# Roots on ACT, residual adds by DMA, a fourth split-weight buffer and a re-ordered norm 2 in a one-core transformer block

## The chip, the cores and the metric

The kernel runs on one core of a Trainium2 chip. The metric is the device time of one execution in microseconds (us); the kernel before was timed in three runs. The engines are called as in the profile: PE multiplies matrices (its weight loads are listed as PEld), DVE does vector work out of on-chip memory and the matmul banks, ACT evaluates functions and copies, POOL does a little arithmetic and issues DMAs that may accumulate into their destination, and SP issues plain DMAs.

## The reference, cut to what matters

512 tokens of 1024 channels, all float32, one layer, one batch entry:

```
h  = rmsnorm(x, norm1_g) * (1 + scale1) + shift1
qa, ka, va, qd, kd, vd, ga, gd = split(h @ w_in)
out_a = sliding-window attention (8 heads, window 128, sinks)
out_d = differential attention (4 heads, two softmax maps), per-head rmsnorm
x  = x + gate1 * ((sigmoid(ga) * (out_a @ w_branch_swa) + sigmoid(gd) * (out_d @ w_branch_diff)) @ w_out)
h2 = rmsnorm(x, norm2_g) * (1 + scale2) + shift2
a, g = split(h2 @ w_up)                 # 1024 -> 2 x 2816
a  = causal conv of width 3 along the tokens, per channel, + conv_b
x  = x + gate2 * ((gelu(a) * g) @ w_down)   # 2816 -> 1024
out = rmsnorm(x, final_g)
```

`scale`, `shift` and `gate` are six rows that come from the conditioning vector `c` (`silu(c) @ w_ada + b_ada`).

## The kernel before, in words

**Split products.** A float32 matrix is multiplied as a high part (a cast to the matmul type, on ACT) and a low part (the difference, on DVE), and each product is three matmuls: high·high, high·low, low·high. So every weight block costs one cast on ACT (line 102 or 990) and one subtraction on DVE (line 103 or 994) before PE can use it. The two parts of a weight lie in rotating buffers with the tags `whi` and `wlo`, `WB` = 3 of each; a new split has to wait until PE is done with the block three before.

**Stages.** In order of time: norm 1 and the first projections (to about 60 us), the two attentions (to 235), the branch projections and gates (to 305), the output projection with norm 2 (to 351), the MLP's up projection (to 578; PE line 1051, matmuls of 128x256), the down projection (to 683.6; PE line 1651, matmuls of 128x512), and the tail.

**Seven products for eight.** Both MLP projections work on a 2 x 2 blocking of their operands with seven block products (p1, m5, m6, p2, m7, p3, p4) of sums of blocks, for eight plain ones. Blocks that are needed as sums are made by DMAs on POOL's queue that accumulate into a loaded block, or by DVE (`sum_w`).

*Up.* `J` counts 11 pairs of column tiles; `mul_slot(J, name)` multiplies one of the seven, `cast_w` and `low_w` split its weight, `behind` takes the result out of its bank, and `conv_taps` and `conv_gelu` do the convolution and GELU. For J = 0 and 1 the order of DVE, ACT, PE and POOL is written out by hand, from the last steps of the output projection on (`out_step`): row by row, `add_x` adds the residual, `square2` sums squares on ACT, `norm_a` and `norm_b` make the root, `norm_c` scales the row; then PE transposes (bank names `th`) and the row is modulated (`early`). The splits of the weights p1 and p2 of pair 1 (`hi_early`, `lo_early`) are placed between these. From J = 2 on a scheduler sets the order.

*Down.* Seven passes over the 2816 channels in six groups (`grp`, five of two tiles and one of one), in the order m1, m5, m6, p2, p3, m7, p4, 66 matmuls each. `prepare(i, g)` splits the weight block and the activation block of a group, and for m1, m5, m6 and p3 then issues an accumulating DMA that turns the weight block (`chain` or `b`) into the one which a later pass needs. In the trace, `b<-in_w_down_dram` on POOL's queue is such a DMA for pass m7: it is issued when p3's split of the same block is done. The results lie in four pairs of banks (dX, dZ, dY, dW). After a pass its results are taken out by small DVE tasks (`after_pass`), handed out over the groups of the next pass by the table `EACH`. p4 accumulates onto dW, the bank that m7 has filled, so its first matmul waits until DVE has taken m7's result out of it (line 1525).

**Residual and last norm.** The tasks multiply by the gate, add into the residual `x1` (`res(t, hf)`: row tile t, half hf) with a DVE addition, sum the squares of the half on ACT (`square`, line 1488), and multiply by the final gain (`fgb`). `stat_start` and `stat_end` make the root of a row.

**Roots.** `rstd_start` raises the mean square to the power −0.5 on POOL (line 143), and `rstd_end` does a refinement step in two DVE operations of 128x1 (lines 149 and 153).

**The tail** (`last_rows`) holds back the last three groups of p4. Row tile 2 is finished first. Then row tile 3 in two halves of 256 columns, `c0` and `c1`, of one bank: all of c0's matmuls, then all of c1's. DVE multiplies by the gate (line 1563), adds (1566), ACT squares (1569), DVE applies the gain (1573), the root follows, and the scaled row goes out in two DMAs, the last one on ACT's queue (1585).

Of the kernel before, what the change touches and what calls it, by code (L numbers as in the profile page):

```python
# [14 lines left out]
P = 128  # L15
# [10 lines left out]
DIFF_HEADS = 4  # L26
WB = 3
HP = 100000
# [15 lines left out]
def kernel(  # L44
# [101 lines left out]
    def rstd_end(dst, ms, r0, n, wpool):  # L146
        t = wpool.tile([P, n], F32, tag="rs_b", bufs=3, name="rt")
        if n == 1:
            nc.vector.scalar_tensor_tensor(t, r0, r0, ms, ALU.mult, ALU.mult)
# [706 lines left out]
    while units or loaded or current or later:  # L856
        fill(1)
    for _ in ada:
        fill(1)
# [259 lines left out]
    def square2(t, hfs=(0, 1)):  # L1119
        for hf in hfs:  # L1120
            sq = big.tile([P, S], F32, tag="sq2", name=f"sqo{t}{hf}")
            ssq[t, hf] = bp.tile([P, 1], F32, tag="ss2", bufs=8, name=f"sso{t}{hf}")
            nc.scalar.activation(sq, x1[:, t, hf * S : (hf + 1) * S], AF.Square, accum_out=ssq[t, hf])  # L1123

    def norm_a(t):
        nc.vector.tensor_scalar(ssq[t, 0], ssq[t, 0], 1.0 / D, EPS, ALU.mult, ALU.add)
        r2[t] = rstd_start(ssq[t, 1], 1, D, bp, plus=ssq[t, 0])

    def norm_b(t):
        rs = bp.tile([P, 1], F32, tag="rs2", bufs=4, name=f"rso{t}")  # L1130
        rstd_end(rs, *r2[t], 1, bp)
        xns[t] = xnp[t // 2][:, t % 2]
        return rs
# [74 lines left out]
    square2(1)  # L1208
    lo_early(2, q0)
    norm_a(1)  # L1210
    lo_early(2, q1)
    norm_c(1, norm_b(1))
# [34 lines left out]
    norm_halves(2, norm_b(2))  # L1247
    norm_halves(3, norm_b(3))
    early(2, "lo")
# [19 lines left out]
    mul_slot(0, "p2", (0,))  # L1269
    cast_w(0, "m5")  # L1270
    for g in (0, 1):
# [7 lines left out]
    bV += [tbank("up6"), tbank("up7")]  # L1279
    low_w(0, "m5")  # L1280
    for q in (q0, q1):
        V.tensor_sub(t1n[:, q], b11[:, q], b12[:, q])
    sum_w(0, "m6")
    hi_t(0, t1n, q0)
# [12 lines left out]
    behind(0, "p1")  # L1297
    nc.scalar.copy(bh[:, 2], b22)
    low_w(0, "m6")
    lo_t(1, t1n, q0)  # L1300
# [32 lines left out]
    mul_slot(1, "m6")  # L1333
    behind(1, "m5")
    conv_bias(0, 1)
    conv_taps(0, 0)
    sum_w(1, "p3")
    conv_taps(0, 1)
    cast_w(1, "p3")
    conv_gelu(0, 0)  # L1340
    behind(1, "m6")
    cast_w(1, "m7")
    low_w(1, "p3")
    mul_slot(1, "p3")
    conv_gelu(0, 1)
    low_w(1, "m7")
    mul_slot(1, "m7")
    load_a(2, 0)
    cast_w(2, "p1")
    behind(0, "c22")  # L1350
    behind(0, "p4")
    behind(1, "p2")
    low_w(2, "p1")
    mul_slot(2, "p1")
    behind(1, "p3")
    cast_w(1, "p4")
    conv_bias(1, 0)
    conv_bias(1, 1)
    low_w(1, "p4")
    behind(1, "m7")  # L1360
    mul_slot(1, "p4")
    load_s1(2)
    load_a(2, 1)
    load_s3(2)
    load_a22(2)
    conv_taps(1, 0)
    cast_w(2, "m5")
    conv_gelu(1, 0)
    low_w(2, "m5")
    sum_w(2, "m6")  # L1370
    behind(2, "p1")
    conv_taps(1, 1)
    cast_w(2, "m6")
    conv_gelu(1, 1)
    low_w(2, "m6")
    behind(1, "c22")
    behind(1, "p4")
    cast_w(2, "p2")
    low_w(2, "p2")
    man.close()  # L1380
# [110 lines left out]
    def stat_start(t):  # L1491
        a, b = parts[t, 0], parts[t, 1]
        nc.vector.tensor_scalar(a, a, 1.0 / D, EPS, ALU.mult, ALU.add)
        parts[t] = rstd_start(b, 1, D, bp, plus=a)

    def stat_end(t):
        rs = bp.tile([P, 1], F32, tag="rs2", bufs=4, name=f"rsd{t}")
        rstd_end(rs, *parts[t], 1, bp)
        return rs
# [4 lines left out]
    def gate(hf):  # L1504
        return g2b[hf]


    def after_pass(name):
# [14 lines left out]
        elif name == "m7":  # L1523
            for u in two:
                yield lambda u=u: V.tensor_sub(e2[:, u], e2[:, u], dW[u])
            for u in two:
                yield lambda u=u: V.tensor_mul(e2[:, u], e2[:, u], gate(1))
            for u in two:
                def add(u=u):
                    V.tensor_add(res(2 + u, 1), res(2 + u, 1), e2[:, u])  # L1530
                    square(2 + u, 1)
                yield add
            for u in two:
                def gain(u=u):
                    V.tensor_mul(e2[:, u], res(2 + u, 1), fgb[:, S:])
                    stat_start(u)
                yield gain
        elif name == "p3":
            for u in two:
                yield lambda u=u: V.tensor_sub(e[:, u], e[:, u], dZ[u])  # L1540
# [21 lines left out]
    def last_mul(u, sl=slice(0, S)):  # L1562
        nc.vector.tensor_mul(m1[:, u, sl], dW[u][:, sl], gate(0)[:, sl])

    def last_add(u, sl=slice(0, S)):
        nc.vector.tensor_add(res(2 + u, 0)[:, sl], res(2 + u, 0)[:, sl], m1[:, u, sl])
        sq = big.tile([P, S], F32, tag="sq2", name=f"sqe{u}_{sl.start}")
        s1 = bp.tile([P, 1], F32, tag="ss2", bufs=8, name=f"sse{u}_{sl.start}")
# [18 lines left out]
    def last_rows(todo):  # L1587
# [53 lines left out]

    def multiply(i, g, u, sl=slice(0, S)):
        name, bank2 = passes[i][:2]
# [3 lines left out]
        for q in range(n):  # L1647
            first_mm = name in first and g == 0 and q == 0
            last_mm = g == len(grp) - 1 and q == n - 1
            for x, (a, b) in enumerate(((ah, wh), (ah, wl), (al, wh))):  # L1650
                nc.tensor.matmul(  # L1651
                    bank2[u][:, sl], a[:, q, cu], b[:, q, sl], start=first_mm and x == 0, stop=last_mm and x == 2,
                    skip_group_check=name not in first,
                )

    NG = len(grp)
    HOLD = 3
    EACH = {3: (0, 2, 2, 2, 1, 1), 4: (0, 0, 1, 1, 2, 2), 5: (0, 0, 2, 2, 2, 2), 6: (0, 0, 2, 2, 2, 2)}
    tasks = iter(())
    for i in range(len(passes)):  # L1660
        for g in range(NG):
            prepare(i, g)
            for _ in range(EACH.get(i, (0,) * NG)[g]):
                next(tasks)()
        tail = HOLD if i == len(passes) - 1 else 0
        for g in range(NG - tail):
            for u in range(2):
                multiply(i, g, u)
        if tail:
# [50 lines left out]
```

## Time and profile before

| | |
|---|---|
| three runs | 693.9 to 696.05 us, median 695.13 |
| profiled execution | 695.11 us, its span 693.3 |
| PE busy | 676.6 us (98%), 4117 matmuls |
| PEld busy | 591.5 us (85%) |
| DVE busy | 559.9 us (81%), 1028 instructions |
| ACT busy | 376.6 us (54%), 661 instructions |
| POOL busy | 72.7 us (10%), 81 instructions |
| DMA | 119.68 MB, mean 173 GB/s |

The busy times are of one execution. DVE's 81% is an average: it has stretches of 10 us in which it is full. In a row of a timeline the first number is the start in us, the second the busy time of the instruction, then engine, line, operation, the output and inputs by the program's names, and in brackets how long the engine stood before it and what released it. Operations on one engine overlap a little, so that the distance of two starts is shorter than the busy time of one.

### The profile page before, as it was taken

To read this page: it belongs to the slowest core of one execution; us is meant where nothing else is said; L and a number is where in the kernel's file an instruction comes from. 1 tells how busy PE (TensorE), PEld (TensorE's weight loads), DVE (VectorE), ACT (ScalarE), POOL (GpSimd) and SP (SyncE) were. 2 spreads that over 40 slices of the span, in tenths; PEclk is the share of its full clock that TensorE was granted. 3 is DMA by queue.
4 is the path that set the end of the run, shared out by engine and by line. 5 is a ranking of instruction groups with operands and counts; after the bars stand their busy time and mean duration, and the time that the engine had idled before them with its cause. 6 is when DMAs were issued, how large, how long until landed. Compare 5 with 4: busy or idle time off the path is not lost. (4 is left out here: it accounts for less than half of the span.)

```text
span 693.3 us, 10915 instructions
## 1 busy us (share of the span) xinstructions
PE 676.6 (98%) x4117; PEld 591.5 (85%) x4117; DVE 559.9 (81%) x1028; ACT 376.6 (54%) x661; POOL 72.7 (10%) x81
## 2 busy tenths in 40 slices
PE   8999999999999999999999999999999999999994
PEld 8787777778787888888799999999999998888873
DVE  4888887879787566663699898888888999979995
ACT  4656765354544333332487655665556565665663
POOL 2000000000100000000030101111111003431200
PEclk9999999999999999999999999999999999999997
DMA  9943544355254464258354988778867558996803
GB/s 351 407 166 108 185 134 151 122 172 158 97 178 156 142 222 152 93 186 245 115 108 133 217 212 197 188 194 185 204 172 185 140 177 204 196 205 182 144 1 122
DMA packets 71077, 119.68 MB, mean 173 GB/s; under 512 B 3952, under 2 KB 47728, under 8 KB 71024
## 3 DMA queue, kind: packets, MB, share of 16 engines
q1 hardware_dynamic: 52960, 95.04, 41.4%
q0 software_dynamic: 17776, 23.60, 20.6%
q8 instruction: 32, 0.52, 0.3%
q10 hardware_dynamic: 288, 0.34, 0.1%
q14 instruction: 21, 0.17, 0.1%
HBM read 116.87 MB, written 2.10 MB: 172 GB/s over the span
## 5 line engine op out<-in xcount | busy, mean ns | idle before, releaser
L1051 PE MATMUL up<-t,m_whi 128*128 128x256 f32 x528 | 96.1, 283 | 0.0
L1051 PEld LDWEIGHTS up<-t,m_whi 128*128 128x128 f32 x528 | 82.3, 192 | 0.0
L1051 PE MATMUL up<-t,m_wlo 128*128 128x256 f32 x264 | 74.6, 283 | 0.1
L1051 PE MATMUL up<-bh,p_wlo 128*128 128x256 f32 x232 | 65.7, 284 | 0.7 <-DVE p_wlo L994 0.7
L1051 PE MATMUL up<-bh,p_whi 128*128 128x256 f32 x232 | 65.6, 283 | 0.0
L1051 PE MATMUL up<-bl,p_whi 128*128 128x256 f32 x232 | 65.6, 283 | 0.0
L673 DVE CUSTOM_DVE_ANT_0 ra<-ra,csb 128x1024 f32<-128x1024 f32 x32 | 39.1, 1223 | 23.5 <-DMA ra<-in_w_ada_t_dram 23.2
L1051 PEld LDWEIGHTS up<-t,m_wlo 128*128 128x128 f32 x264 | 50.6, 192 | 0.3 <-DVE m_wlo L994 0.3
L1051 PEld LDWEIGHTS up<-bh,p_wlo 128*128 128x128 f32 x232 | 44.4, 192 | 1.1 <-DVE p_wlo L994 1.1
L1051 PEld LDWEIGHTS up<-bh,p_whi 128*128 128x128 f32 x232 | 44.5, 192 | 0.0
L1051 PEld LDWEIGHTS up<-bl,p_whi 128*128 128x128 f32 x232 | 44.5, 192 | 0.0
L962 POOL DMA_DIRECT2D s<-in_w_up_dram x21 | 27.1, 1363 | 156.0 <-DMA s<-in_w_up_dram 109.4
L143 POOL TENSOR_TENSOR r<-ms,mhalf 128x1 f32<-128x1 f32 (+1 forms) x13 | 11.8, 910 | 297.9 <-DVE ms L139 220.8
L994 DVE TENSOR_TENSOR m_wlo<-s,m_whi 128x1024 fp32r<-128x1024 f32 x31 | 37.8, 1220 | 2.0 <-ACT m_whi L990 2.0
L990 ACT CAST m_whi<-s 128x1024 fp32r<-128x1024 f32 x31 | 32.4, 1046 | 9.3 <-DVE s L984 6.0
L612 ACT ACTIVATE sd<-sd,dmx 128x128 f32<-128x128 f32 (+3 forms) x32 | 17.8, 556 | 29.8 <-DVE dmx L610 24.0
L1051 PE MATMUL up<-t,p_whi 128*128 128x256 f32 x176 | 32.2, 283 | 0.0
L1051 PEld LDWEIGHTS up<-t,p_whi 128*128 128x128 f32 x176 | 27.4, 192 | 0.2 <-issue 0.2
L1058 ACT ACTIVATE gT<-a,cols 128x512 f32<-128x512 f32 x22 | 17.7, 813 | 17.7 <-DVE a L1093 17.3
L990 ACT CAST p_whi<-wa 128x1024 fp32r<-128x1024 f32 x18 | 18.7, 1041 | 12.0 <-DMA s<-in_w_up_dram 8.9
L1051 PE MATMUL up<-t,p_wlo 128*128 128x256 f32 x88 | 24.9, 283 | 0.0
L994 DVE TENSOR_TENSOR p_wlo<-wa,p_whi 128x1024 fp32r<-128x1024 f32 x18 | 22.0, 1222 | 3.5 <-ACT p_whi L990 3.0
(497 smaller groups left out, 2010.0 us busy)
## 6 DMA issues: line engine op xcount, KB each, us to landing
ra<-in_w_ada_t_dram SPq DMA_DIRECT2D x32, 512.0 KB, 3.3
wa<-in_w_up_dram SPq DMA_DIRECT2D x22, 512.0 KB, 4.4
s<-in_w_up_dram SPq DMA_DIRECT2D x21, 512.0 KB, 4.7
s<-in_w_up_dram POOLq DMA_DIRECT2D x21, 512.0 KB, 6.1
adaw<-in_w_ada_t_dram SPq DMA_DIRECT2D x15, 512.0 KB, 9.8
a<-in_w_up_dram SPq DMA_DIRECT2D x11, 512.0 KB, 4.8
b<-in_w_down_dram SPq DMA_DIRECT2D x10, 512.0 KB, 4.3
w<-in_w_first_dram SPq DMA_DIRECT2D x8, 512.0 KB, 10.1
```

The costliest lines, as they stand in the source:

```text
L143: nc.gpsimd.tensor_tensor(r0, ms, mhalf[:, :n], ALU.pow)
L612: nc.scalar.activation(pm[m], pm[m], AF.Exp, bias=mx[:, m : m + 1], scale=slope, accum_out=lsum[:, m : m + 1])
L673: nc.vector.tensor_tensor_reduce(r, r, csb, 1.0, 0.0, ALU.mult, ALU.add, late_mod[:, idx : idx + 1])
L962: nc.gpsimd.dma_start(dst, upblock(*blk), accum_op=ALU.add)
L990: nc.scalar.copy(W[J, name][0], R[J, SRC[name]])
L994: nc.vector.tensor_sub(lo, R[J, SRC[name]], hi.bitcast(F32))
L1051: nc.tensor.matmul(o[u], w[:, k, cu], b[:, k], start=name in ("p1", "m5", "p2") and k == 0 and x == 0, stop=k == 3 and x == 2, skip_group_ ...
L1058: nc.scalar.activation(grow(j), av[J][:, u], AF.Identity, bias=cv[:, 66 + j : 67 + j], scale=cv[:, 44 + j : 45 + j])
```

## The change

- `WB` goes from 3 to 4: a fourth buffer for the high and the low part of split weights. The memory is taken from the area in which POOL's DMAs keep their descriptors (`dynamic_dma_scratch_size=8192`, which is 16384 without the argument).
- Roots of norm 2, of the last norm's rows and of the tail: ACT's Sqrt, then a reciprocal on DVE, for the power on POOL; the refinement step stays. Two more functions' tables are asked for ahead of time by a Sqrt or Gelu of one column (`root_table`, `warm`): Sqrt behind the last tanh of the gates, Gelu behind norm 2, Sqrt ahead of the down projection.
- Ahead of norm 2: the split of weight m5 of pair 0 and the second early cast come before the output projection's last steps; `lo_early(2)` is moved up by one row, and the sum for m6 takes its place. Further down in the hand-written order, casts, splits, convolution and GELU of J = 0 to 2 change places.
- Down projection: six residual additions of 128x512 on DVE (two each after p2, p3 and m7) become accumulating DMAs on POOL's queue from on-chip memory into `x1`; the square on ACT and the gain on DVE follow the DMA. After m7, two `row` tasks scale and send out the rows 0 and 1, which was done in the tail. The last groups of m7 and the first of p4 are multiplied one row tile at a time (`together`).
- Tail: the second half of row tile 3 is multiplied into a bank of its own (dY[1]); multiplications, additions, gain and scaling are ordered anew.

```diff
-WB = 3
+WB = 4
+    def root_start(ssq, d, wpool, plus):
+        r0 = wpool.tile([P, 1], F32, tag="rs_c", bufs=3, name="r0")
+        nc.scalar.activation(r0, ssq, AF.Sqrt, bias=plus, scale=1.0 / d)
+        ms = wpool.tile([P, 1], F32, tag="rs_a", bufs=3, name="ms")
+        nc.vector.scalar_tensor_tensor(ms, ssq, 1.0 / d, plus, ALU.mult, ALU.add)
+        return ms, r0
+
+    def root_end(dst, ms, r0, wpool):
+        nc.vector.reciprocal(r0, r0)
+        rstd_end(dst, ms, r0, 1, wpool)
+
+    def root_table(behind):
+        nc.scalar.activation(warm, behind, AF.Sqrt, scale=0.0)
...
+    root_table(tds[KT - 1][:, 0:1])
...
     hi_early(1)
     lo_early(1, slice(0, 4))
+    cast_w(0, "m5")
+    low_w(0, "m5")
+    hi_early(2)
     for k in last:
         out_step(0, k)
     add_x(0, 0)
     add_x(0, 1)
     square2(0)
+    lo_early(2, q0)
     norm_a(0)
+    lo_early(2, q1)
     norm_c(0, norm_b(0))
-    hi_early(2)
     for k in last:
         out_step(1, k)
     add_x(1, 0)
     add_x(1, 1)
     square2(1)
-    lo_early(2, q0)
+    sum_w(0, "m6")
     norm_a(1)
-    lo_early(2, q1)
     norm_c(1, norm_b(1))
...
     nc.scalar.copy(bh[:, 2], b22)
+    nc.scalar.activation(warm, rs_last, AF.Gelu, scale=0.0)
...
+    root_table(grow(FT - 1)[:, 0:1])
...
                 def add(u=u):
-                    V.tensor_add(res(2 + u, 1), res(2 + u, 1), e2[:, u])
+                    nc.gpsimd.dma_start(res(2 + u, 1), e2[:, u], accum_op=ALU.add)
                     square(2 + u, 1)
...
+            for u in two:
+                def row(u=u):
+                    nc.scalar.activation(x1[:, u], x1[:, u], AF.Copy, scale=stat_end(u))
+                    nc.sync.dma_start(od[u * P : (u + 1) * P, :], x1[:, u])
+                yield row
...
                 def add(u=u):
-                    V.tensor_add(res(u, 1), res(u, 1), e[:, u])
+                    nc.gpsimd.dma_start(res(u, 1), e[:, u], accum_op=ALU.add)
                     square(u, 1)
...
                 def add(u=u):
-                    V.tensor_add(res(u, 0), res(u, 0), m1[:, u])
+                    nc.gpsimd.dma_start(res(u, 0), m1[:, u], accum_op=ALU.add)
                     square(u, 0)
...
-        for sl in (c0, c1):
-            for g in todo:
-                multiply(len(passes) - 1, g, 1, sl)
-        for u in range(2):
-            nc.scalar.activation(x1[:, u], x1[:, u], AF.Copy, scale=stat_end(u))
-            nc.sync.dma_start(od[u * P : (u + 1) * P, :], x1[:, u])
-        last_mul(0)
-        s0 = last_add(0)
-        last_gain(0)
-        last_mul(1, c0)
-        r0 = rstd_start(s0, 1, D, bp, plus=part[0])
-        s1 = last_add(1, c0)
-        last_gain(1, c0)
+        for g in todo:
+            multiply(len(passes) - 1, g, 1, c0)
+        for g in todo:
+            multiply(len(passes) - 1, g, 1, c1, dY[1], g == todo[0])
+        last_mul(0, dW[0])
+        last_add(0)
+        s0 = last_square(0)
+        last_mul(1, dW[1])
+        r0 = root_start(s0, D, bp, part[0])
         rs0 = bp.tile([P, 1], F32, tag="rs2", bufs=4, name="rse0")
-        rstd_end(rs0, *r0, 1, bp)
+        root_end(rs0, *r0, bp)
+        last_add(1)
+        last_scale2(0, rs0, nc.sync)
+        s1 = last_square(1, c0)
+        nc.vector.scalar_tensor_tensor(res(2, 0), res(2, 0), rs0, fgb[:, :S], ALU.mult, ALU.mult)
+        nc.sync.dma_start(od[2 * P : 3 * P, :S], res(2, 0))
+        last_mul(1, dY[1], c1)
+        last_add(1, c1)
+        s2 = last_square(1, c1)
         partial(s1, part[1])
-        last_mul(1, c1)
-        s2 = last_add(1, c1)
-        r1 = rstd_start(s2, 1, D, bp, plus=s1)
-        last_gain(1, c1)
-        last_scale(0, rs0)
-        last_scale2(0, rs0, nc.sync)
+        last_gain(1)
+        r1 = root_start(s2, D, bp, s1)
         rs1 = bp.tile([P, 1], F32, tag="rs2", bufs=4, name="rse1")
-        rstd_end(rs1, *r1, 1, bp)
+        root_end(rs1, *r1, bp)
...
-    EACH = {3: (0, 2, 2, 2, 1, 1), 4: (0, 0, 1, 1, 2, 2), 5: (0, 0, 2, 2, 2, 2), 6: (0, 0, 2, 2, 2, 2)}
+    EACH = {3: (0, 2, 2, 2, 1, 1), 4: (0, 0, 1, 1, 2, 2), 5: (0, 0, 2, 2, 2, 2), 6: (0, 0, 2, 2, 3, 3)}
...
+        together = {"m7": (4, 5), "p4": (0, 1)}.get(passes[i][0], ())
         for g in range(NG - tail):
             for u in range(2):
-                multiply(i, g, u)
+                for gg in together if g in together[:1] else () if g in together else (g,):
+                    multiply(i, gg, u)
```

More of the change, by code (lines that the diff above doesn't have):

```diff
@@ L1123, in square2 @@
             nc.scalar.activation(sq, x1[:, t, hf * S : (hf + 1) * S], AF.Square, accum_out=ssq[t, hf])
+            if hf == 0:
+                nc.vector.tensor_scalar(ssq[t, 0], ssq[t, 0], 1.0 / D, EPS, ALU.mult, ALU.add)
     def norm_a(t):
[L1126 to L1127 removed]
+        r2[t] = root_start(ssq[t, 1], D, bp, ssq[t, 0])
     def norm_b(t):
         rs = bp.tile([P, 1], F32, tag="rs2", bufs=4, name=f"rso{t}")
[L1131 removed]
+        root_end(rs, *r2[t], bp)
         xns[t] = xnp[t // 2][:, t % 2]
@@ L1365 @@
     load_a22(2)
-    conv_taps(1, 0)
-    cast_w(2, "m5")
+    cast_w(2, "m5")
+    low_w(1, "p4")
+    behind(1, "m7")
+    conv_bias(1, 0)
+    conv_bias(1, 1)
+    low_w(2, "m5")
+    mul_slot(1, "p4")
+    sum_w(2, "m6")
+    conv_taps(1, 0)
+    cast_w(2, "m6")
+    low_w(2, "m6")
+    behind(2, "p1")
+    cast_w(2, "p2")
+    low_w(2, "p2")
     conv_gelu(1, 0)
-    low_w(2, "m5")
-    sum_w(2, "m6")
-    behind(2, "p1")
     conv_taps(1, 1)
-    cast_w(2, "m6")
     conv_gelu(1, 1)
-    low_w(2, "m6")
     behind(1, "c22")
     behind(1, "p4")
-    cast_w(2, "p2")
-    low_w(2, "p2")
     man.close()
@@ L1640, in prepare, with multiply @@
         ops[i, g] = ah, al, wh, wl
-    def multiply(i, g, u, sl=slice(0, S)):
+    def multiply(i, g, u, sl=slice(0, S), o=None, fresh=False):
         name, bank2 = passes[i][:2]
@@ L1647, in multiply @@
         for q in range(n):
-            first_mm = name in first and g == 0 and q == 0
+            first_mm = (name in first and g == 0 or fresh) and q == 0
             last_mm = g == len(grp) - 1 and q == n - 1
@@ L1651, in multiply @@
                 nc.tensor.matmul(
-                    bank2[u][:, sl], a[:, q, cu], b[:, q, sl], start=first_mm and x == 0, stop=last_mm and x == 2,
-                    skip_group_check=name not in first,
+                    (bank2[u] if o is None else o)[:, sl], a[:, q, cu], b[:, q, sl], start=first_mm and x == 0, stop=last_mm and x == 2,
+                    skip_group_check=name not in first and o is None,
                 )
```

36 lines of the change are left out of this document (15 added, 21 removed).

## The prediction

> **What bounds the kernel now.** I read the page first: busy times, then the chain that ended last; after it the table by stretch for the stages that the change touches, the list of waits, and the timelines of the down projection and the tail.
>
> ```profile
> PE 676.6 (98%) x4117; PEld 591.5 (85%) x4117; DVE 559.9 (81%) x1028; ACT 376.6 (54%) x661; POOL 72.7 (10%) x81
> ...
> 393.81 184.34 PE up L1051 x1534
> 578.15 89.12 PE dc L1651 x393
> 667.29 0.70 DVE chain_outl L1525
> 668.13 15.45 PE dc L1651 x81
> ```
>
> PE works in 98% of the 693.3 us of the span, and from 393.81 to the tail the chain is PE alone, but for one DVE operation at 667.29. The change takes no matmul away. So it can win only where PE stands or behind its last matmul, 668.13 + 15.45 = 683.58, and it can lose wherever a moved wait comes ahead of PE. The time outside of the span is 695.11 − 693.3 = 1.8 us. The profiled execution took 695.11 us and the median is 695.13, so the sum needs no correction. About 0.3% (2.1 us) is what a measurement of this kernel can tell from no change.
>
> **The split of norm 2 and the first MLP slots.** The table by stretch (start:end, length, then PE, PEld, DVE, ACT, POOL busy with instruction counts, clock, DMA share, GB/s) and PE's waits there:
>
> ```profile
> 360.00:370.00 10.00, 10.00 (x86) 10.00 (x85) 10.00 (x13) 8.15 (x16) 0.00 (x0) 1.00 0.92 193
> 370.00:380.00 10.00, 10.00 (x85) 10.00 (x85) 10.00 (x12) 7.04 (x11) 1.29 (x1) 1.00 0.27 82
> 380.00:390.00 10.00, 9.64 (x79) 9.27 (x77) 7.92 (x11) 7.27 (x12) 1.28 (x1) 1.00 0.98 250
> 390.00:400.00 10.00, 9.56 (x78) 9.16 (x77) 9.93 (x19) 5.08 (x8) 1.68 (x2) 1.00 0.81 174
> ```
>
> ```profile
> PE up L1051 <- DVE p_wlo L994: 0.7, 2, 0.3
> PE th L1146 <- DVE xn L1136: 0.7, 1, 0.7
> PE th L1146 <- ACT braw L1156: 0.2, 1, 0.2
> ```
>
> DVE is full from 360 to 380. Where PE doesn't stand it starts 85 or 86 matmuls in 10 us, 0.118 us each; in 380 to 400 it starts 157 where 169 would fit: 12 × 0.118 = 1.4 us lost, more than the 0.7 that the list of waits names. With the two waits of the transposes, 0.9, PE loses 2.3 here. The change moves ahead of norm 2 one cast and one subtraction of a split (m5 of pair 0) and one weight sum (m6): two DVE operations of 128x1024, 1.14 apart in the rows further below, 2.3 us out of the very stretch in which DVE is full. That is as much as PE loses. I take −2.3. Bounds: −1.4 (the transposes' waits stay, since the moved pieces now stand ahead of norm 2's own work on DVE) and −2.6 (0.3 more, about what the 9.64 busy in 380 to 390 leaves idle).
>
> **Attention and the fourth buffer.** PE's waits from 60 to 305 us:
>
> ```profile
> PE tp L526 <- ACT pT L528: 1.1, 1, 1.1
> PE td L627 <- DVE sd L618: 0.8, 1, 0.8
> PE sw L113 <- DVE mx L492: 0.6, 1, 0.6
> ```
>
> None of these ends on a split weight buffer; each ends on softmax work. The buffer lets the splits run one group further ahead of PE, which reorders that work but removes none. I take 0, with the largest wait either gone or come a second time: −1.1 to +1.1.
>
> **Roots on ACT.** The power on POOL becomes a Sqrt on ACT and a reciprocal on DVE. That needs Sqrt's table after the last tanh, Gelu's after norm 2 and Sqrt's again ahead of the down projection: three loads for one.
>
> ```profile
> 385.63 1.28 ACT L1066 ACT_TABLE_LOAD   x1
> 386.92 0.63 ACT L1066 ACTIVATE gT<-gT 128x512 f32<-128x512 f32 x1
> 575.13 1.53 ACT L1058 ACTIVATE gT<-a,cols 128x512 f32<-128x512 f32 x2 [1.62 <-DVE a L1093]
> ```
>
> One load costs ACT 1.28 us and its next work starts at once, 0.01 behind it. ACT is busy 54% of the span and stands 1.62 at 575; the Gelu load moves into 360 to 370, where ACT has 10 − 8.15 = 1.85 idle. I take 0: this idle time is the cover. Without it a load would cost 1.3 in the norm or down stage, +1.3 at most for one that stands in the chain. The Trainium skill, ScalarE: Activation LUTs, section What ACT_TABLE_LOAD costs, speaks against switching sets: it puts about 1283 ns of load and a drain of about 1380 ns on each switch; its load agrees with the row here (1.28), its drain doesn't show in it (0.01). By the skill's total two more switches would be an estimated 5.3 us of ACT time, still not on PE's path by the idle time above.
>
> **The tail.** Rows behind the last matmul:
>
> ```profile
> 683.60 0.42 DVE L1563 TENSOR_TENSOR pairs<-dc,g2row 128x256 f32<-128x256 f32 x1 [1.44 <-PE dc L1651]
> 685.37 0.41 DVE L1563 TENSOR_TENSOR pairs<-dc,g2row 128x256 f32<-128x256 f32 x1
> 686.34 0.42 ACT L1569 ACTIVATE sqe<-x 128x256 f32<-128x256 f32 x1 [1.25 <-DVE x L1566]
> 687.18 0.62 POOL L143 TENSOR_TENSOR r<-ms,mhalf 128x1 f32<-128x1 f32 x1 [2.30 <-DVE ms L141]
> 687.84 0.22 DVE L149 SCALAR_TENSOR_TENSOR rt<-r,ms 128x1 f32<-128x1 f32 x1
> 689.04 0.35 ACTq L1585 DMA_DIRECT2D out_dram<-x  x1
> ```
>
> Now DVE stands 1.44 us until 683.60 for the whole bank, although its first half was multiplied before the second, and only then does that half; the second half's multiply starts at 685.37 and the last output DMA 3.67 later. After the change the second half lies in a bank of its own, so the first half's work fills the wait. The second half's 15 matmuls take 15 × 0.12 = 1.8, so the first half is complete at 681.8; multiply and add of 128x512 (0.6 each by the rows below), three or four tiny operations (0.5) and a scaled product (0.6) follow and end at 684.1, so the second half starts 685.37 − 684.1 = 1.3 earlier. Behind it POOL's 0.62 and its handing over go, for a Sqrt and a reciprocal of 128x1 on two engines, about 0.4 (two small operations); the gain multiply grows from 128x256 to 128x512, 0.3. So −1.3 − 0.2 + 0.3 = −1.2. Bounds −0.8 (the root on two engines takes as long as POOL) and −1.5 (the gain is hidden under the root).
>
> **The down projection.** Six residual adds leave DVE: each becomes a 256 KB accumulating DMA on POOL's queue, followed by a Square on ACT that waits for its landing. What is queued behind each: on POOL the weight blocks that accumulate for pass m7 (b); on ACT the next casts; on DVE the gain product of the same row. POOL's new order is b0, b1, add, b2, b3, add, b4, b5, and ACT's has the second add's Square ahead of m7's first cast. The rows:
>
> ```profile
> 622.42 0.69 DVE L1516 TENSOR_TENSOR chain_kvB<-dc,pairs 128x512 f32<-128x512 f32 x1 [0.49 <-PE dc L1651]
> 637.08 1.20 POOL L1637 DMA_DIRECT2D b<-in_w_down_dram  x1 [18.23 <-DVE p3a L103]
> 648.05 0.91 POOL L1637 DMA_DIRECT2D b<-in_w_down_dram  x1 [0.61 <-DVE p3wl L103]
> ```
>
> ```profile
> 637.00:639.00 2.00, 2.00 (x11) 1.65 (x10) 1.62 (x2) 2.00 (x3) 1.20 (x1) 1.00 0.01 1
> 639.00:655.00 16.00, 16.00 (x72) 13.27 (x71) 14.57 (x23) 10.59 (x18) 5.72 (x5) 1.00 1.04 180
> ```
>
> ```profile
> 644.46 0.62 ACT L1488 ACTIVATE sqd<-x 128x512 f32<-128x512 f32 x1
> 644.99 0.18 ACT L1488 ACTIVATION_READ_ACCUMULATOR sqd<-x 128x1 f32 x1
> 648.93 1.05 ACT L102 CAST m7wh<-b 128x1024 fp32r<-128x1024 f32 x1 [1.58 <-PE dc L1651]
> 650.02 1.23 DVE L103 TENSOR_TENSOR m7wl<-b,m7wh 128x1024 fp32r<-128x1024 f32 x1 [0.94 <-ACT m7wh L102]
> 652.82 0.39 PE L1651 MATMUL dc<-m7wh,m7a 128*128 128x512 f32 x1
> 652.94 1.22 DVE L103 TENSOR_TENSOR m7wl<-b,m7wh 128x1024 fp32r<-128x1024 f32 x1
> 654.08 0.68 DVE L1540 TENSOR_TENSOR chain_kvB<-chain_kvB,dc 128x512 f32<-128x512 f32 x1
> 654.68 1.22 DVE L103 TENSOR_TENSOR m7wl<-b,m7wh 128x1024 fp32r<-128x1024 f32 x1
> 667.29 0.69 DVE L1525 TENSOR_TENSOR chain_outl<-chain_outl,dc 128x512 f32<-128x512 f32 x1 [0.29 <-PE dc L1651]
> 668.13 0.47 PE L1651 MATMUL dc<-p4wh,p4a 128*128 128x512 f32 x1 [0.19 <-DVE chain_outl L1525]
> ```
>
> The clock is that of before. Six b blocks, five of 512 KB and one of 256, go at 180 GB/s with the DMA engines full: 0.524 MB / 180 GB/s = 2.9 us each. The first moves 1.9 behind its issue (637.08 to 639).
>
> First b: DVE does it as soon as its queue allows. From 622.42 the new queue holds 12 operations of 128x512 at 0.60 apart, four of 128x1024 at 1.14 and one of 0.4: 12.2, so b0 is issued at 634.6, and its data flow from 636.5. The second add is the sixth in the line: 4 × 2.9 + 2 × 1.45 = 14.5, if an add from on-chip memory moves as fast as b does. It lands at 651.0. Square and read-out 0.7, cast 1.05, subtraction 1.22 with small handovers: m7wl of the first group is done at 654.2, where it was done at 650.02 + 1.23 = 651.25. PE reaches m7 at 652.82 and stands some 1.4 us.
>
> Then p4. Its first matmul waits for DVE's subtraction out of the same bank (667.29, done 667.98, PE 0.15 later). Between m7wl and that subtraction's end DVE has 15 operations of 0.60, six of 1.14, one of 0.4 and ten tiny ones of about 0.1: 17.2, so 671.4. ACT can be later: the second m7-stage add is issued at 662.2, its stream behind the first's ends at about 665.8 (661.25 + 1.6 + 2 × 1.45; 1.6 since the issue of 256 KB takes 0.91 for 1.20); Square 0.7, cast 1.05, subtraction 1.22, then 3.4 of DVE work: 672.1. I take the later, so p4 starts at 672.25 for 668.13: **+4.1**. Bounds: 0 (adds land in time) and +7.3 (below). The earlier standing at m7 is inside it.
>
> **Sum.** 695.11 − 2.3 + 0 + 0 − 1.2 + 4.1 = **695.7 us**.
>
> **Rivals.** First: the adds are hidden. For it: their source is on chip, and the trace has no such transfer. Six blocks were issued within 11 us (637.08 to 648.05); the second add is the sixth of eight, so by 634.6 + 11 × 5/7 = 642.5 (an estimate). If it queues behind nothing it lands 1.6 + 1.45 later, 645.5, ahead of the cast that stood at 648.93, and 4.1 goes: 691.6, faster. Against it: the share of 1.04 over 16 us says that the queue is full. By the Trainium skill, DMA: Bandwidth & Descriptors, section Anatomy of one DMA — SWDGE (gpsimd) path, a DMA takes 2.0 us and its bytes at 436 GB/s. By that rule (an estimate) a block would need 1.2 us and nothing would wait; the 180 GB/s measured here speaks against it.
>
> Second, on the other side: an add costs more than its bytes. At 2.2 us for each 256 KB (half as much again) the second add lands 1.5 later, 652.5, and m7wl is done at 655.7; the pair for p4 is issued at 662.7 and 663.7 and ends at 668.7, and Square, cast, subtraction and the 3.4 give 675.1: p4 starts 7.1 to 7.3 late, 698.9 in all. It decides from where an add lands after about 652. For it: ACT stands on the landing and has casts behind it twice. Against it: nothing in the trace is that slow for its bytes.
>
> Third: the splits ahead of norm 2 do not win, because norm 2's vector work comes later by as much as the first slots win: 698.0 with the adds waiting, 693.9 without.
>
> **How the numbers follow.** Forecast 0.42, first rival 0.36, second 0.16, third 0.06. The forecast's own range is 693.2 to 698 (the loss between 2 and 6); of its 0.42, 0.05 is faster, 0.26 the same, 0.11 slower. The first gives 0.34 faster, 0.02 same; the second is slower; the third 0.01, 0.02 and 0.03. Faster 0.40, same 0.30, slower 0.30. Two signs hold most of the chance, so the range reaches from the first rival with the bounds of its terms (691.6 − 0.8) to the second: 690.8 to 698.9.
>
> **What would show it.** Right: in 380 to 400 at least 165 matmuls start; m7's first cast stands behind a Square that a DMA released; p4 starts three to five us later against m6's end than before; from the last matmul to the last output DMA some 4.3 us for 5.5. Wrong: the Square's landing lies ahead of 648 on the clock of before (first rival), or a PE wait of over 2 us in a stage that I put at 0.

## The result, and the profile after

The changed kernel takes 700.72 us (median of four runs, 699.2 to 702.75) against 694.51 for the kernel before: a ratio of 1.0091, 95% interval 1.0066 to 1.0116. It is slower by some 6 us; the forecast was 695.7 with a range up to 698.9. The profiled execution took 699.2 us, with a span of 697.4: 4.1 more than the 693.3 of before.

First the page, then PE's waits in the list of waits (what waited and for whom, us in total, times, longest):

```profile
PE 676.2 (97%) x4117; PEld 589.6 (85%) x4117; DVE 554.5 (80%) x1028; ACT 381.4 (55%) x674; POOL 73.4 (11%) x79
...
PE dc L1677 <- DVE chain_outl L1544: 3.8, 1, 3.8
PE pga L106 <- ACT ta L697: 2.2, 1, 2.2
...
PE dc L1677 <- DVE m7wl L103: 0.8, 1, 0.8
PE dc L1677 <- ACT m7wh L102: 0.5, 1, 0.5
```

The change did what it says: DVE has 5.4 us less to do. PE has the same work and new waits: 3.8 at the start of p4, 1.3 at the start of m7, and 2.2 in attention at a gate's bank (`pga`) that none of the forecast's terms named.

The down projection, from the timelines of ACT, POOL, DVE and PE:

```profile
650.79 0.63 ACT L1507 ACTIVATE sqd<-x 128x512 f32<-128x512 f32 x1 [4.37 <-DMA x<-pairs]
651.42 1.03 ACT L102 CAST m7wh<-b 128x1024 fp32r<-128x1024 f32 x1
664.41 0.63 ACT L1507 ACTIVATE sqd<-x 128x512 f32<-128x512 f32 x1 [3.92 <-DMA x<-chain_kvB]
665.89 0.63 ACT L1507 ACTIVATE sqd<-x 128x512 f32<-128x512 f32 x1 [0.43 <-DMA x<-chain_kvB]
666.52 1.03 ACT L102 CAST p4wh<-chain_kvA 128x1024 fp32r<-128x1024 f32 x1
677.93 0.63 ACT L1507 ACTIVATE sqd<-x 128x512 f32<-128x512 f32 x1 [3.17 <-DMA x<-chain_outl]
678.66 1.05 ACT L102 CAST p4wh<-chain_outh 128x1024 fp32r<-128x1024 f32 x1
```

```profile
633.90 1.20 POOL L1663 DMA_DIRECT2D b<-in_w_down_dram  x1 [18.60 <-DVE p3wl L103]
661.03 1.75 POOL L1569 DMA_DIRECT2D x<-chain_kvB  x2 [12.78 <-DVE chain_kvB L1566]
```

```profile
652.49 1.23 DVE L103 TENSOR_TENSOR m7wl<-b,m7wh 128x1024 fp32r<-128x1024 f32 x1 [0.18 <-ACT m7wh L102]
671.79 0.68 DVE L1544 TENSOR_TENSOR chain_outl<-chain_outl,dc 128x512 f32<-128x512 f32 x1
```

Three times ACT stands at a Square until a residual add has landed, and each time a cast for PE is right behind it: m7's first at 651.42, p4's first at 666.52, that of p4's fifth group at 678.66. That is the forecast's chain. PE then starts p4 at 672.61:

```profile
672.61 0.47 PE L1677 MATMUL dc<-p4wh,p4a 128*128 128x512 f32 x1 [3.78 <-DVE chain_outl L1544]
672.92 0.58 PE L1677 MATMUL dc<-p4wl,p4a 128*128 128x512 f32 x1
673.29 1.06 PE L1677 MATMUL dc<-p4wh,p4a 128*128 128x512 f32 x2
674.15 0.63 PE L1677 MATMUL dc<-p4wl,p4a 128*128 128x512 f32 x1
```

The matmuls behind that stall start 0.43 us apart, where they start 0.227 apart otherwise. The table by stretch shows why (the column with 0.56 is the clock granted to PE):

```profile
668.00:672.00 4.00, 0.84 (x4) 0.37 (x2) 3.93 (x9) 4.00 (x7) 0.00 (x0) 1.00 0.09 35
672.60:676.50 3.90, 3.89 (x10) 3.12 (x11) 3.90 (x5) 2.16 (x4) 0.86 (x1) 0.56 0.82 239
676.50:680.40 3.90, 3.90 (x18) 3.19 (x18) 2.71 (x5) 2.46 (x5) 0.86 (x1) 1.00 0.40 69
```

A stall of 3.8 us cost PE its full clock for the 3.9 behind it: 10 matmuls for 18. The Trainium skill, TensorE: Matmul & The Clock Gate, section Part 1: The HAM clock gate (the "warmup" mystery), says that PE falls to half its clock after an idle window of about 3.4 us and stays there for about as long; 0.43 us here agrees with its 426.7 ns for a matmul of 512 columns, and 3.9 × (1 − 0.56) = 1.7 us lost are 3.4 us at half the clock. Its idle window doesn't agree with every run: further below, stalls of 2.1 and 2.2 us are followed by the half clock too.

Norm 2's first slots and the tail:

```profile
380.00:390.00 10.00, 10.00 (x86) 10.00 (x85) 9.05 (x14) 6.47 (x11) 0.88 (x2) 1.00 0.96 253
390.00:400.00 10.00, 10.00 (x85) 10.00 (x84) 9.84 (x18) 5.53 (x9) 1.92 (x2) 1.00 0.90 180
```

```profile
689.37 0.28 PE L1677 MATMUL dc<-p4wh,p4a 128*128 128x256 f32 x1
690.49 0.41 DVE L1587 TENSOR_TENSOR pairs<-dc,g2row 128x256 f32<-128x256 f32 x1
692.00 0.29 ACT L157 ACTIVATE r<-sse,sse 128x1 f32<-128x1 f32 x1
693.72 0.35 ACTq L1611 DMA_DIRECT2D out_dram<-x  x1
```

In 380 to 400 PE starts 171 matmuls for 157 and never stands. The last output DMA comes 693.72 − 689.65 = 4.1 us behind the last matmul, 5.5 before.

The account by stage, from the start of the first matmul of each stage in the timelines (attention: first `sw` to first product of the output projection; then to the first matmul of pass m1; then to the end of the last matmul, of which p4; then to the end of the span), in us, one profiled execution each:

| kernel | start | attention | norm 2, MLP | down | of which p4 | end | span |
|---|---|---|---|---|---|---|---|
| before | 62.17 | 243.48 | 272.34 | 105.57 | 15.43 | 9.8 | 693.3 |
| changed | 60.57 | 245.97 | 270.46 | 112.65 | 17.04 | 7.8 | 697.4 |
| changed, again | 61.13 | 246.54 | 270.36 | 112.43 | 17.01 | 7.8 | 698.3 |
| adds_dve | 60.69 | 247.86 | 270.04 | 105.12 | 15.33 | 7.8 | 691.5 |
| adds_p2_dve | 60.89 | 247.52 | 270.27 | 106.42 | 15.42 | 7.8 | 692.9 |
| adds_p3_dve | 60.97 | 247.85 | 269.94 | 109.18 | 15.40 | 7.8 | 695.7 |
| adds_m7_dve | 60.84 | 247.71 | 270.11 | 112.14 | 17.05 | 7.8 | 698.6 |
| adds_m7_dve_warm | 60.97 | 248.11 | 270.14 | 111.09 | 15.43 | 7.8 | 698.1 |
| after_warm | 61.30 | 248.61 | 270.05 | 112.74 | 17.19 | 7.8 | 700.5 |
| before_wb4 | 61.07 | 248.05 | 271.45 | 105.58 | 15.44 | 9.3 | 695.4 |
| before_area8 | 61.17 | 243.96 | 273.25 | 105.62 | 15.44 | 9.8 | 693.8 |
| three_dve | 61.00 | 243.57 | 273.67 | 105.24 | 15.40 | 8.3 | 691.7 |
| three_dve_pool | 60.82 | 243.32 | 274.44 | 105.20 | 15.40 | 9.0 | 692.8 |
| own_m5 | 61.14 | 243.29 | 275.95 | 105.15 | 15.36 | 8.3 | 693.8 |
| tail_only | 60.79 | 243.44 | 272.26 | 105.19 | 15.40 | 8.3 | 690.0 |
| four_late | 61.25 | 243.95 | 270.75 | 105.15 | 15.36 | 8.2 | 689.3 |

Between the first two rows: −1.6 at the start, +2.5 in attention, −1.9 in norm 2 and the MLP, +7.1 in the down projection, −2.0 at the end: +4.1. The start isn't the change: every other kernel profiled, the small edits of before among them, has 60.6 to 61.3, so before's one profiled execution was late there. How far one execution can be trusted shows in before_area8, which has before's order: it took 0.9 more in norm 2 and the MLP. Eight of the sixteen profiles lose 1.7 us, one of them twice, to a stretch of half clock behind a stall of PE: the changed kernel's two and adds_m7_dve in p4; adds_dve, adds_m7_dve, after_warm and before_wb4 in attention; own_m5 and three_dve_pool in norm 2.

### The profile page after: what moved, and what is told of

Read it like the earlier page. It is cut to its first block, busy times and chain, and to the rows that moved or that the text cites. A ratio compares the mean times of both kernels' runs of the same rounds, so it can differ in the third digit from the quotient of the medians.

```text
span 697.4 us, 10916 instructions
## 1 busy us (share of the span) xinstructions
PE 676.2 (97%) x4117; PEld 589.6 (85%) x4117; DVE 554.5 (80%) x1028; ACT 381.4 (55%) x674; POOL 73.4 (11%) x79
## 4 chain that ended last, share of the span: by engine, by line
PE 63%; DVE 16%; DMA 8%; issue 6%; ACT 4%; POOL 2%; SPq 0%; POOLq 0%; ACTq 0%; DVEq 0%
PE up L1066 32%; PE dc L1677 8%; DMA ra<-in_w_ada_t_dram 5%; DVE ra L687 2%; PE pgd L108 2%; PE pgd L106 2%; PE pgd L107 2%; DVE adaw L246 2%; ACT sd L626 1%; PE oc L1122 1%; PE oc L1126 1%; PE oc L1123 1%; DMA wa<-in_w_up_dram 1%; DVE w_l L103 1%; PE pga L106 1%
## 5 line engine op out<-in xcount | busy, mean ns | idle before, releaser
L143 POOL TENSOR_TENSOR r<-ms,mhalf 128x4 f32<-128x4 f32 x5 | 6.3, 1263 | 221.0 <-DVE ms L139 199.6
L999 DVE TENSOR_TENSOR s<-s,wa 128x1024 f32<-128x1024 f32 x20 | 24.4, 1218 | 0.1
```

Of the source, the lines that this page charges most:

```text
L999: nc.vector.tensor_add(src, src, R[J, "a11" if name == "m6" else "a12"])
```

## The experiments

**One part of the residual adds undone at a time.** `adds_dve` puts all six on DVE, the others the pair of one pass:

```diff
-                    nc.gpsimd.dma_start(res(u, 0), m1[:, u], accum_op=ALU.add)
+                    V.tensor_add(res(u, 0), res(u, 0), m1[:, u])
```

> All six residual adds go back to DVE; the rest of the change stays. Theory (a Square on ACT that waits for an accumulating DMA stands ahead of the next pass's first cast): the stalls at m7 (0.68 + 1.03 us) and p4 (3.94) go to under 1 in all, no p4 matmul runs at 0.43 us for 0.227 any more (1.7 us), so about 700.7 - 6.7 = 694.0. Rival 1 (DVE, with 6 x 0.6 = 3.6 us more work, is late for p4 in their place): a stall of 1.5 to 2.5 at p4 stays, 695.5 to 696.5. Rival 2 (the fourth buffer and the new order in attention cost the time): stays above 698.

Measured 693.52, ratio to before 0.9983 (0.9968 to 0.9998). PE has no stall over 0.1 us left in the down projection. So the adds by DMA cost some 7 us, and DVE has room for the 3.6 that they save it.

> Only p2's two adds (in pass p3, ahead of m7's first cast) go back to DVE. Theory: the stall at m7 goes (1.7); m7's first low part is done some 3 us earlier, so p4's stall shrinks from 3.9 to about 1.5 and the half-speed matmuls behind it go (1.7): about 700.7 - 1.7 - 2.4 - 1.7 = 694.9. Rival (p3's adds alone make p4 late, by their own landing): m7's stall goes, p4's stays above 3, 699.

Measured 695.52, ratio 1.0007 (0.9991 to 1.0022). m7's stall is gone, p4's is 1.1, and p4 takes its 15.4: as the theory had it.

> Only p3's two adds (in pass m7, ahead of p4's first cast) go back to DVE. Theory (p4 is late mainly because DVE and ACT start pass m7 late behind p2's adds): DVE gains the 1.36 us that it waits for the landings and pays 1.2 for the adds, so p4's stall stays above 3 and the time at 700 +- 0.7. Rival (p4's lateness is that of p3's adds): p4's stall under 2, no half-speed matmuls, 697 or less.

Measured 698.76, ratio 1.0067 (1.0044 to 1.0091): between theory and rival, and the eight runs lie in two groups, five at 697.5 to 699.4 and three at 701.3 to 701.5. The profiled one is of the first:

```profile
672.54 0.47 PE L1677 MATMUL dc<-p4wh,p4a 128*128 128x512 f32 x1 [2.44 <-DVE ms L159]
672.84 0.40 PE L1677 MATMUL dc<-p4wl,p4a 128*128 128x512 f32 x1
673.08 0.62 PE L1677 MATMUL dc<-p4wh,p4a 128*128 128x512 f32 x2
```

The stall is 2.44 and the matmuls behind it come at full speed. What the slow group has on top is not shown; no run of it was profiled. The clock granted to PE over the whole span is on record for every run: 0.992 to 0.995 in the three, 0.995 to 0.998 in the five. That would fit stretches of half clock, behind this stall or elsewhere.

**Does the half clock cost the 1.7 us?** `after_warm` gives PE something to do in p4's stall:

```diff
+        if tail:
+            for _ in range(15):
+                nc.tensor.matmul(dY[0][:, :P], ones, ones, start=True, stop=True)
```

> The changed kernel with 15 idle matmuls (128x128, some 0.2 us each, 3.2 us in all) into a free bank between pass m7 and pass p4, where PE stands 3.9 us anyway; the output is unchanged. Theory (PE's matmuls come at half their rate after a stall as long as p4's, because PE stood): with PE busy in most of that time p4's first nine matmuls come 0.227 apart and not 0.43, so 1.7 us less, 699.0, with p4's start where it was. Rival (they are slow because of what p4 reads, weights or banks that DVE and ACT use at the same time): still 0.43, 700.7 or a little more.

Measured 701.89, ratio 1.0092 (1.0073 to 1.011): nothing gained. Yet the clock did what the theory said:

```profile
675.51 0.47 PE L1677 MATMUL dc<-p4wh,p4a 128*128 128x512 f32 x1 [0.51 <-DVE chain_outl L1544]
675.81 0.40 PE L1677 MATMUL dc<-p4wl,p4a 128*128 128x512 f32 x1
676.05 0.63 PE L1677 MATMUL dc<-p4wh,p4a 128*128 128x512 f32 x2
...
685.74 0.50 PE L1677 MATMUL dc<-p4wh,p4a 128*128 128x512 f32 x1 [0.42 <-ACT p4wh L102]
687.00 0.50 PE L1677 MATMUL dc<-p4wl,p4a 128*128 128x512 f32 x1 [0.76 <-DVE p4wl L103]
```

PE starts p4 at the full rate, and 10 us later it waits for the fifth group's cast, which stands behind the Squares of both of m7's adds:

```profile
680.04 0.64 ACT L1507 ACTIVATE sqd<-x 128x512 f32<-128x512 f32 x1 [2.39 <-DMA x<-chain_outl]
684.02 0.63 ACT L1507 ACTIVATE sqd<-x 128x512 f32<-128x512 f32 x1 [3.26 <-DMA x<-chain_outl]
684.56 0.19 ACT L1507 ACTIVATION_READ_ACCUMULATOR sqd<-x 128x1 f32 x1
684.65 1.03 ACT L102 CAST p4wh<-chain_outh 128x1024 fp32r<-128x1024 f32 x1
```

What the clock gives, that wait takes. But with the idle matmuls in the program the scheduler also chose another order on ACT. In the changed kernel the second Square comes behind these casts, not ahead of them (ACT, then DVE's low part of the fifth group):

```profile
681.13 0.63 ACT L1507 ACTIVATE sqd<-x 128x512 f32<-128x512 f32 x1 [0.54 <-DMA x<-chain_outl]
679.75 1.23 DVE L103 TENSOR_TENSOR p4wl<-chain_outh,p4wh 128x1024 fp32r<-128x1024 f32 x1 [1.12 <-ACT p4wh L102]
```

There the group is ready 680.98 − 672.61 = 8.4 us behind p4's first matmul; `after_warm`'s PE, at the full rate, asks for it 685.32 − 675.51 = 9.8 behind. So in the changed kernel's own order it would not have been late at the full clock either: the late cast is `after_warm`'s own. Two runs bear on this: m7's adds on DVE without and with the idle matmuls.

> Only m7's two adds (in pass p4) go back to DVE. The run with idle matmuls ahead of p4 took the half speed away, but 1.7 us came back as waits at p4's fifth group, whose cast stands behind the Square of m7's first add. Theory (two causes lie side by side: nine matmuls at 0.43 us, and the late cast; each alone costs the 1.7): taking one away gives nothing, so the time stays at 700.5 +- 0.8 with p4 still at half speed for its first matmuls. Rival (the late cast alone costs it): 699 or less.

Measured 700.73, ratio 1.0095 (1.0079 to 1.0111): no gain by itself; p4 takes 17.05, eight of its matmuls at half speed. ACT has the fifth group's cast ahead of both Squares here, and PE has no wait in p4, so the half clock is p4's only loss.

> m7's two adds on DVE and the 15 idle matmuls ahead of p4, both. Theory (as for adds_m7_dve): with both causes gone p4 takes 15.5 us from its first to its last matmul as in the kernel before, and the kernel is 1.6 us faster than with one: 699.0. Rival (something third holds p4 up): p4 takes 17 us, 700.7.

Measured 698.74, ratio 1.0067 (1.0046 to 1.0087); p4 takes 15.43. Against adds_m7_dve the median falls by 2.0; the two intervals overlap, so it is p4's own time that carries the argument: 17.05 falls to 15.43. So the half clock alone costs 1.6 in p4, and in `after_warm` a cast that the new order made late took as much. That both causes lie in the changed kernel and each hides the other, as I had expected, the rows don't bear out.

**The fourth buffer alone**, put into the kernel before:

```diff
-WB = 3
+WB = 4
-    nc = _bacc.Bacc("TRN2", target_bir_lowering=False, num_devices=1)
+    nc = _bacc.Bacc("TRN2", target_bir_lowering=False, num_devices=1, dynamic_dma_scratch_size=8192)
```

> The kernel before with four buffers for split weights in place of three and the smaller descriptor area, nothing else. Theory (the fourth buffer reorders the splits in attention, where the changed kernel lost 2.5 us between 62 and 305 us): 696 to 697, with PE stalls in attention above the 3.2 us of before. Rival (that loss belongs to the single execution profiled, not to the buffer): 694.5 +- 0.7.

Measured 696.62, ratio 1.0026 (1.0012 to 1.0041). It loses 4.6 us in attention, gains 0.9 in norm 2 and 0.5 at the end. The list of waits has the changed kernel's wait, which before doesn't have; then ACT's timeline, of before_wb4 and of before:

```profile
PE pga L106 <- ACT ta L683: 2.2, 1, 2.2
```

```profile
191.74 1.05 ACT L102 CAST wga_h<-wga 128x1024 fp32r<-128x1024 f32 x1 [0.51 <-PE pga L107]
195.07 0.40 ACT L612 ACTIVATE sd<-sd,dmx 128x128 f32<-128x128 f32 x1 [2.28 <-DVE dmx L610]
196.84 0.57 ACT L683 ACTIVATE ta<-pga 128x512 f32<-128x512 f32 x1
```

```profile
191.47 1.06 ACT L102 CAST wba_h<-wba 128x1024 fp32r<-128x1024 f32 x1 [2.51 <-PE pga L107]
192.43 0.59 ACT L683 ACTIVATE ta<-pga 128x512 f32<-128x512 f32 x1
```

In both, a cast stands behind the finished gate bank, with a free buffer that of another weight. In before, the operation that empties the bank (`ta`) is next, 1.0 us behind the cast's start; in before_wb4 it goes behind four exponentials that wait for DVE, 5.1 us behind the cast's start, and PE needs the bank. That names 2.2 of the 4.6. Another 1.7 is half clock: the table by stretch just behind that stall, of before_wb4 and of the changed kernel, which has the same stall there:

```profile
197.90:201.30 3.40, 3.40 (x10) 2.62 (x9) 3.40 (x6) 0.93 (x1) 0.00 (x0) 0.51 0.28 113
196.90:200.30 3.40, 3.40 (x18) 2.78 (x17) 3.40 (x6) 0.96 (x2) 0.00 (x0) 1.00 0.31 120
```

Of the nine profiles with this stall of 2.2 us, four have the half clock behind it and five do not, so the length of a stall doesn't decide it alone. The 0.7 that is left I didn't part.

> The kernel before with the descriptor area halved to 8 KB and three buffers. Theory (the fourth buffer itself, by the order that it lets the scheduler choose, made the kernel before 2.2 us slower): no change, 694.4 +- 0.7. Rival (the small area holds up POOL's DMAs): the 2.2 us or part of it are here, 695.5 to 696.6.

Measured 694.72, ratio 0.9996 (0.9983 to 1.0009). The smaller descriptor area costs nothing; it is the buffer.

**Three buffers with the rest.** `three_dve` has three buffers and all adds on DVE, and puts these three back to their old places:

```diff
-    cast_w(0, "m5")
-    low_w(0, "m5")
...
-    sum_w(0, "m6")
```

> Three split buffers and the full descriptor area as before, the six adds on DVE, the early split of m5 and the early sum for m6 put back where they were; tail, roots on ACT and the other moves stay. Theory (the fourth buffer costs some 4.5 us between 62 and 305 us, of which the start gives 1 to 1.5 back; the adds on DVE cost nothing): attention as before (243.5 us from the first sw to the first oc product), tail 2.0 shorter, something between 0 and 0.9 in norm 2: 692.0, between 691.5 and 692.5. Rival (the gain of norm 2 and the down projection needs the buffer, and the attention's loss doesn't come from it): 693.5 or more.

Measured 694.79, ratio 1.0002 (0.9989 to 1.0015): the rival's number. Attention is as before, the end 1.5 shorter, but norm 2 and the MLP take 273.7 for before's 272.3 (273.3 in before_area8).

> As three_dve, but all roots by the power on POOL as before, and one table load in place of three. Theory (a root on ACT saves in the tail about 0.4 us and its table loads are hidden): 0.3 to 0.6 slower than three_dve. Rival (the loads of Sqrt's and Gelu's tables cost in the norm and MLP stages): 0.5 to 2 us faster than three_dve.

Measured 694.74, ratio 1.0002 (0.9991 to 1.0013): no difference to roots on ACT that could be measured. In the profiles its end is 0.8 longer (9.0) and its norm 2 and MLP 0.8 longer too, but 1.7 of the latter is half clock, at 348 behind a stall of 2.1 at the transposes, so one execution of each can't settle it. Roots and table loads together change nothing that shows.

`own_m5` keeps all moves of norm 2 with three rotating buffers, and gives m5 of pair 0 a pair of its own:

```diff
+        own = (J, name) == (0, "m5")
         W[J, name] = [
-            wp.tile([P, 4, 256], F32R, tag=g, bufs=WB, name=f"{name}_{J}_{g}") for g in ("whi", "wlo")
+            big.tile([P, 4, 256], F32R, tag="own" + g, name=f"{name}_{J}_{g}") if own
+            else wp.tile([P, 4, 256], F32R, tag=g, bufs=WB, name=f"{name}_{J}_{g}") for g in ("whi", "wlo")
```

> Three rotating split buffers, but the early split of m5 (pair 0) in a pair of its own in the memory of the fourth; all six adds on DVE; norm 2, roots and tail as changed. Theory (the fourth rotating buffer loses 4.4 us in attention because the scheduler then puts casts earlier; the moves in norm 2 need only one more pair): from the first sw to the first oc product 243.5 as before, for 247.9 with four, norm 2 and the MLP 270 to 271 (272.3 before), tail 7.8 to 8.3: 689.5, between 688.8 and 691. Rival (the norm-2 gain needs four rotating buffers): 692 to 693.

Measured 694.73, ratio 1.0008 (0.9996 to 1.002): a miss by 5 us. Attention is 243.3 as expected, norm 2 and the MLP 276.0, 3.6 over before: the wait at the transposes is 2.5 longer (3.2 for 0.7), and the half clock behind it costs 1.7. From its list of waits, its table by stretch and DVE's timeline, and then DVE's of adds_dve (four rotating buffers, the same written order):

```profile
PE th L1164 <- DVE xn L1154: 3.2, 1, 3.2
```

```profile
350.90:354.30 3.40, 3.40 (x12) 2.69 (x11) 2.74 (x7) 3.37 (x9) 0.00 (x0) 0.55 0.25 86
```

```profile
335.36 1.22 DVE L103 TENSOR_TENSOR wo_l<-wo,wo_h 128x1024 fp32r<-128x1024 f32 x1
339.49 1.23 DVE L1210 TENSOR_TENSOR early<-wa,early 128x1024 fp32r<-128x1024 f32 x1 [2.91 <-ACT early L1206]
```

```profile
332.02 1.23 DVE L103 TENSOR_TENSOR wo_l<-wo,wo_h 128x1024 fp32r<-128x1024 f32 x1 [1.66 <-ACT wo_h L102]
335.08 1.23 DVE L1208 TENSOR_TENSOR early<-wa,early 128x1024 fp32r<-128x1024 f32 x1 [1.83 <-ACT early L1204]
```

The two kernels reach the output projection at 304.43 and 308.55, so by their own stage the last weight split ends 7.5 us later with three buffers, and the pieces that were moved ahead of norm 2 come behind it. This says that the moves need the buffer, not for m5 but for the lead of the splits before it; `four_late` below puts that to the test.

**The tail alone**: the kernel before with the changed down projection and tail, all adds on DVE, three buffers.

> The kernel before up to the end of the MLP's up projection; only the down projection's roots on ACT, its row tasks, the order of m7's and p4's last and first groups and the tail are those of the change, with all adds on DVE and three buffers. Theory (the tail is worth 1.5 to 2.0 us by itself, and the p4 stall of 0.35 goes): 692.4 +- 0.5. Rival (the tail's gain is undone by DVE, which has the row tasks and the roots on top): 693.8 or more.

Measured 691.76, ratio 0.9965 (0.9953 to 0.9977): faster than both kernels.

**Buffer and gain parted.** `four_late` has three buffers through attention; from the output projection's weights on, every fourth split goes into a pair of its own; the adds are on DVE, the rest is the change.

```diff
+    def late_pair(shape, name):
+        turn[0] += 1
+        own = turn[0] % 4 == 0
+        return [
+            wp.tile(shape, F32R, tag="own" + g, bufs=1, name=f"{name}_{g}") if own
+            else wp.tile(shape, F32R, tag=g, bufs=WB, name=f"{name}_{g}") for g in ("whi", "wlo")
+        ]
```

> Three split buffers through attention and four from the output projection's weights on (every fourth split goes into a pair of its own); all six adds on DVE; the rest of the change as it is. Theory (the fourth buffer loses its 4.4 us in attention only, and norm 2's gain needs it at the output projection, where with three the moved pieces hold up wo's splits): first sw to first oc product 243.5, from there to the down projection 270 to 270.5, down projection and tail as in adds_dve: adds_dve's span of 691.5 less 4.4, so 689.1 in all, between 688.5 and 690. Rival (the lateness of attention's splits returns as a stall later, or norm 2's gain needs the buffer earlier): 691 to 693.

Measured 691.25, ratio 0.9951 (0.9934 to 0.9968): the fastest of all against its own runs of before. The two effects part as expected (243.95 and 270.75). But the time lies in the rival's range: every stage but the down projection came out 0.4 to 0.7 over what I had put, 2 us in all. In norm 2 PE stands 1.2 at the transposes, for 0.5 in adds_dve. Whether it beats `tail_only` the intervals don't tell.

> The changed kernel once more, for a second profile. Theory (the 2.5 us that its profiled execution lost in attention is the low end, since seven other profiled kernels with four buffers lost 3.4 to 5.1): 4 to 4.8 lost between the first sw and the first oc product, a time above 700. Rival (the changed kernel loses only 2.5 there): 245.9 us for that stretch, as in the first profile.

Measured 700.04, with 246.54 in attention: nearer to the rival. Nine profiled executions with four buffers have 246.0 to 248.6 there, seven with three 243.3 to 244.0. The changed kernel's own two are the lowest of the nine, though its order in attention is that of adds_dve (247.9). Four of the other seven have the half clock behind the stall at the gate's bank, which the changed kernel's two profiles don't have; less its 1.7 they would have 246.0 to 246.9. The other three stand longer elsewhere (4.9 to 6.4 us in all by their lists of waits, for 3.9 and 4.5 in the changed kernel's two); what lengthens those waits is open.

## Why the prediction was wrong, step by step

- **Norm 2 and first MLP slots, −2.3.** Right: −1.9, and −2.0 and −2.3 in two other profiles; 171 matmuls where I asked for 165. What I hadn't seen is that it hangs on the fourth buffer: with three, part of the moves wins nothing (three_dve has 273.7, before's order 272.3 and 273.3) and all of them lose 3.6 (own_m5), 1.7 of it by the half clock.
- **Attention and the fourth buffer, 0 ± 1.1.** This step failed: +2.5 and +3.1 in the changed kernel's profiles, +4.6 in before with the buffer alone. I argued that none of PE's waits ended on a split buffer, so that the new order of the softmax work would come to nothing. But a free buffer changes what the scheduler puts next on ACT, and work that is due then comes late: PE stands 2.2 at a gate's bank, and in four of nine profiles, none of them the changed kernel's, pays 1.7 of half clock on top.
- **Roots on ACT, 0.** Right, as far as 0.3% tells.
- **Tail, −1.2.** The mechanism was right: −1.4 to the last output DMA, −2.0 to the end of the span.
- **Down projection, +4.1.** The mechanism was right at each place, and the adds' stream came 0.8 later than worked out: m7's Square was released at 650.79, on the clock of before (1.0 more) 651.8 for 651.0. m7 lost 1.7 (0.7 ahead of its first matmul and 1.0 ahead of its second, by their starts; I had 1.4). From the first matmul of m1 to p4's first it was +5.5: the pair of adds for p4 landed 1.1 later than in my sum (its issue alone came 0.8 behind the 661.25 there, for which the sum gives no row), and what stands between the landing and p4 took 0.3 longer.
- **p4 itself.** Missing from the sum: I let p4 take its 15.4 us once it had started. It took 17.0, since PE's clock was halved behind the stall that I had forecast. The third pair of adds holds up the fifth group's cast too, but PE doesn't stand for it.
- **The account.** Against the forecast's 695.7 the profiled execution has +2.5 (attention), +1.4 (p4's start), +1.6 (p4), +0.4 (norm 2), −0.8 (end) and −1.6 (start): 699.2. The median is 1.5 above that execution, which was the fastest of the four; what the slower ones had on top, the half clock in attention or something else, is not shown.
- **The rivals.** The second, an add that costs more than its bytes, got near the time for another reason: the pair's landings are 1.48 apart (664.41, 665.89), as 180 GB/s has it. The first fell with m7's stall. The 0.30 for slower was too low: p4's term was missing and could only cost, and I gave a change to the order on ACT bounds of equal size on both sides.

## What to carry to other kernels

A wait for a DMA on an in-order engine costs what is queued behind it, so look for the next pass's first operation before giving an add to a DMA queue, even when the engine that is relieved is busy 80% of the time. When a forecast holds a stall of PE of two us or more, put 1.7 us of half clock behind it as a possible cost, near four us as an expected one (all three here had it), and if you fill the stall, look at what the scheduler does to the order on the other engines. And a deeper buffer in front of a scheduler isn't free: try it by itself, and where it loses in one stage and wins in another, give it to the one stage alone.

## What the runs showed of the hardware that I had not expected

PE's granted clock fell to 0.56 in the 3.9 us behind a stall of 3.8, and eight to nine matmuls came 0.43 apart; where idle matmuls filled such a stall, they came 0.227 apart. From the first `sw` to p4's start the sixteen profiles have three stalls of 3.8, all with the half clock behind them; thirteen of 2.1 to 3.2, six with it and seven without, on both sides the same stall of 2.2 at the same place; and none with it of 1.6 or less. What decides between 2.1 and 3.2 is open. An accumulating DMA of 256 KB between two places on chip landed 3.4 us after its issue, and the next one 1.48 later, at the same 180 GB/s as blocks from outside.
